# Order of the head-pair projections, and where the stick-breaking output norm takes its squares, in a hybrid attention trunk on one core

## The chip, the core and the metric

The kernel runs on one core of a Trainium2 chip. A core has a matrix engine (PE, with its weight loads shown apart as PEld), a vector engine (DVE), a scalar engine (ACT), a general engine (POOL), and queues that start transfers (most of them SP's). The metric is the time of one execution on the chip in microseconds (us), here the median of three runs.

## The reference

One layer of a streaming encoder works on T = 1088 tokens (1024 of a prompt, 64 of a sample with 128 cached ones). What matters here:

```python
h = rmsnorm(x, g_mix) * (1.0 + scale) + shift            # b_ada, w_ada give scale, shift
q_sb, k_sb, v_sb, q_fx, k_fx, v_fx, logf = split(h @ w_in)  # 8 heads of 64 of each kind
# stick-breaking heads (no softmax)
a = exp(log_sigmoid(z) + cumsum_reverse(log_keep) - log_keep);   o_sb = a @ v_sb
# forgetting heads
p = softmax(mask(q_fx @ k_fx.T / 8 + fq - fk));                  o_fx = p @ v_fx
o = concatenate([rmsnorm(o_sb, g_sb_out), rmsnorm(o_fx, g_fox_out)])   # 512 columns each
x = x + (1.0 + ada[2]) * (o @ w_o)
# then a SwiGLU feed-forward block, a second residual and a last norm
```

The outputs are the new x, the new keys and values of both kinds of heads, and the forget gates. All is in float32.

## The kernel before

**Tiles.** Every float32 operand of a matmul is held as a high and a low part, and a product is three matmuls (L429 high by high, L430 high by low, L431 low by high). Tokens go in three chunks (0 to 383, 384 to 767, 768 to 1087). Heads go in pairs: pairs 0 to 3 are stick-breaking, 4 to 7 forgetting, so that the "sixth pair" is pair index 5.

**A pair.** `project_pair` makes q, then k, then v of a pair (3 chunks x 8 slices of 128 x 3 matmuls each), copies k out for the cache result and its transposes (L501, L507, L512), and returns the raw rows. `values` splits v. `setup` makes of one head the parts the scores take (k2 and kl of k, qs and q2 of q; L572 and L574 are subtractions on POOL).

**Attention.** `attention` takes, for each head and each of nine query blocks, one or two parts of up to 512 keys: the scores (`ps_z`, L689, L692, the mask at L696), for a forgetting head the row maximum (DVE, L717), its negative (L723, L726), the exponential (ACT, L729, which first needs an ACT_TABLE_LOAD where another function was in use), the sum and reciprocal (DVE, L732, L733), the division (POOL, L735), the transposes (PE, `pt_a`, L744), their high part (ACT, L443) and low part (DVE, L750), the product with v (PE, `ps_av`, L753), a fold (DVE, `ot`, L661) and a store to the scratch `oT_d` (SP, L663). A stick-breaking head has two sigmoids (L704), a scan (L708) and a multiplication (POOL, L712) in the place of the softmax. The tiles `a_t`, `o_lo` and the new `o_sq` share one ring of six buffers.

**The stick-breaking norm.** The outputs of pairs 0 to 3 lie in `oT_d` in two halves, since the high and the low part of v give each a sum. `low_job` runs beside each pair; at pair 5 it calls `o_stats` for the three chunks, which loads both halves, adds them (POOL, L824), squares them (ACT, L825) and sums the squares into `sqacc` (POOL, L827, L830). After the first head of pair 6, `sb_early` turns all sums into one column of reciprocal roots (`token_cols`, with matmuls at L204 and a Sqrt at L191, for which ACT loads another table), and calls `sb_norm` for chunks 0 and 2: spread the column over the partitions (L223), load the halves a second time, add them (POOL, L836), scale them (DVE, L900). `sb_ready`, at the start of the attention of pair 7, does chunk 1, splits all three and lets the output projection (`acc_o`, L429 to L431) begin beside the last pair's attention. `squares` (L812) is the sum of squares of the second group norm.

**Order.** The attention of pair n is written ahead of the projections of pair n+1. A list scheduler then sets each engine's order of instructions from a simulated time line; it moves projection matmuls between attention matmuls wherever these would wait. The feed-forward block, from about 850 us, has an order of its own that the change does not touch. Loads and stores sit in SP's queue in the order that the scheduler gives them.

Of the kernel before, what the change touches and what calls it, by code (L numbers as in the profile page):

```python
# [8 lines left out]
F32 = mybir.dt.float32  # L9
# [7 lines left out]
P = 128  # L17
# [72 lines left out]
def f32(ap):  # L90
    return ap.bitcast(F32)
# [3 lines left out]
def tile_hybrid_trunk(  # L95
# [90 lines left out]
    def bank(tag, name):  # L186
        return ps.tile([P, 512], F32, tag=tag, bufs=bank_bufs[tag], name=name)
# [84 lines left out]
    def t_lowraw(dt=F32):  # L272
        return ap1.tile([P, 4, 256], dt, tag="lowraw", name="lowraw")
# [175 lines left out]
    def load_cols(c0):  # L449
        raw, hi, lo = load_w(col_block(w_in[0], c0), KT, P)  # L450
        split(raw, hi, lo, act, pool if c0 in LCP else eng[E_LC[c0 >= 1536]])
        return hi, lo

    def pair_cols(pr):
        return (1536 if pr >= 4 else 0) + (pr % 4) * P

    def load_qk(pr):
        return load_cols(pair_cols(pr)), load_cols(pair_cols(pr) + 512)

    def project(w, evac, tags):  # L460
# [13 lines left out]
    def project_pair(pr, wq, wk):  # L474
        fox = pr >= 4
        p4 = pr % 4
        ck = cache_fox_k if fox else cache_sb_k
        kp, ks = (fox_k_p, fox_k_s) if fox else (sb_k_p, sb_k_s)
        cs = slice(p4 * P, (p4 + 1) * P)
        ptags = PT if pr == 0 else ("acc",) * 9  # L480
        qraw = t_raw(f"qraw{pr}")
        kraw = t_raw(f"kraw{pr}")
        vraw = t_raw(f"vraw{pr}")

        def q_evac(c, t0, n, acc):
            (act.activation(qraw[:, t0:t0 + n], acc[:, :n], AF.Copy, scale=0.125) if E_QE == 'a' else dve.tensor_scalar(out=qraw[:, t0:t0 + n], in0=acc[:, :n], scalar1=0.125, scalar2=None, op0=ALU.mult))

        def k_evac(c, t0, n, acc):
            for a, b, d in kcols(c, t0, n):
                cp(E_KE, kraw[:, d:d + b - a], acc[:, a:b])  # L490

        def v_evac(c, t0, n, acc):
            cp(E_VE, vraw[:, t0:t0 + n], acc[:, :n])

        project(wq, q_evac, ptags[0:3])
        project(wk, k_evac, ptags[3:6])
        wv = load_cols(pair_cols(pr) + 1024)
        kc = ap2.tile([P, P], F32, tag="kc", name="kc")
        sync.dma_start(out=kc, in_=ck[0, 0].rearrange("t h d -> t (h d)")[:, cs])
        pt = bank("acc", "pt_kc")  # L500
        pe.transpose(out=pt[:, 0:P], in_=kc, identity=ident)  # L501
        dve.tensor_copy(out=kraw[:, NP:NP + PAST], in_=pt[:, 0:P])
        kv = kp[0, 0].rearrange("(j p) h d -> p j (h d)", p=P)
        for j0, nj in ((0, 4), (4, 4), (8, 1)):
            pt, st = bank("u", "pt_r"), t_st("kst")
            if nj == 1:
                pe.transpose(out=pt[:NS, 0:P], in_=kraw[:, NP + PAST:KW], identity=ident)  # L507
                act.copy(out=st[:NS, 0:P], in_=pt[:NS, 0:P])
                sync.dma_start(out=ks[0, 0].rearrange("t h d -> t (h d)")[:, cs], in_=st[:NS, 0:P])
                continue  # L510
            for j in range(nj):
                pe.transpose(out=pt[:, j * P:(j + 1) * P], in_=kraw[:, (j0 + j) * P:(j0 + j + 1) * P], identity=ident)  # L512
            cp(E_KS[fox], st, pt)
            sync.dma_start(out=kv[:, j0:j0 + nj, cs], in_=st.rearrange("p (j c) -> p j c", j=nj))
        project(wv, v_evac, ptags[6:9])
        return qraw, kraw, vraw

# [42 lines left out]
            pool.memset(f32(vv[hb][NS:P, 9, :]), 0.0)  # L560
        return vv

    def setup(pr, hb, qraw, kraw, vv):
# [19 lines left out]
        return qs, k2, kl, q2, vv[hb]  # L583

    def forget_gates():

# [224 lines left out]
            act.activation(s_, o[i], AF.Square)  # L811
            add.tensor_tensor(out=acc, in0=acc, in1=s_, op=ALU.add)  # L812

    def o_stats(c, acc):

        t0, n = CH[c]
        for i in range(0, 4, 2):
            both = [
                t_.rearrange("p a b -> p (a b)")[:, 0:2 * n].rearrange("p (k t) -> p k t", k=2)
                for t_ in (t_lowraw(), f32(ap1.tile([P, 4, 256], F32R, tag="ada_l", name="sq_l")))]  # L820
            for k in range(2):
                load_o([t_[:, k] for t_ in both], i + k, t0, n)
            sq = both[0]
            pool.tensor_tensor(out=sq, in0=sq, in1=both[1], op=ALU.add)  # L824
            act.activation(sq, sq, AF.Square)  # L825
            if i == 0:
                pool.tensor_tensor(out=acc, in0=sq[:, 0], in1=sq[:, 1], op=ALU.add)  # L827
            else:
                for k in range(2):
                    pool.tensor_tensor(out=acc, in0=acc, in1=sq[:, k], op=ALU.add)  # L830

    def sum_o(o, k, t0, n, add):

        lo = t_z("o_lo")[:, 0:n]
# [21 lines left out]
    def out_block(g, mp, chunks, hi, lo, evac, tags):  # L856

        wh, wl = wo.pop((g, mp)) if (g, mp) in wo else load_wo(g, mp)
        for c in chunks:
            for m in (2 * mp, 2 * mp + 1):  # L860
# [16 lines left out]
    sb_o = [None] * 3
    sqacc = []
    cols_sb = ap1.tile([P, 2, 9], F32, name="cols_sb")

    def sb_early():

        token_cols([sqacc[0]], [(a, min(P, T - a)) for a in range(0, T, P)], 512, cols_sb)
        for c in SBE:
            sb_norm(c, SBT[c])

    def sb_norm(c, tag):

# [13 lines left out]
        sb_o[c] = o
# [7 lines left out]
    def low_job(pr):  # L910

        for job in JOBS[pr]:
            ada_job(job)
        if pr != 5:
            return lambda: None
        sqacc.append(t_low("sqacc"))
        for c, (t0, n) in enumerate(CH):
            o_stats(c, sqacc[0][:, t0:t0 + n])

        return lambda: None  # L920


    fxh = [[None] * 3 for _ in range(4)]
# [61 lines left out]
        sb_norm(1, SBT[1])  # L985
        sb_split(1)

    low_finish = low_job(0)
    hooks = {6: {0: sb_early}, 7: {HK[0]: fox_first, HK[1]: fox_second}}
    for pr in range(8):  # L990
        if pr < 7:
            wqk = load_qk(pr + 1)
        if pr == 7:
            sb_ready()
        attention(pr, heads, hooks.get(pr, {}))
        if pr < 7:
# [3 lines left out]
            low_finish()  # L1000
# [631 lines left out]
```

## Time and profile before

| | |
|---|---|
| median of three runs | 1619.83 us (1618.46 to 1623.54) |
| the profiled execution | 1622.84 us |
| its span, first to last instruction | 1621.0 us |
| mean granted clock of PE | 0.983 of full speed |
| PE busy | 1537.0 us, 95% |
| DVE, ACT, POOL busy | 1076.9, 782.2, 734.3 us |

The profiled execution takes 1.8 us beyond its span. PE is busy nearly all of the time as a whole, so time is lost only in the stretches where it is not, and a table of windows is the way to them: for each stretch its length, the busy time of every engine with the number of instructions, the clock granted to PE, and the share of the transfer engines. The last product of pair 6's v ends at 587.1 us, the first one of pair 7 begins at 650.4; pair 7's last v product ends at 703.9, and the output projection's first begins at 712.0.

### The profile page before, as it was taken

How to read it: one execution, taken by the hardware profiler on the slowest of the kernel's cores; microseconds unless marked ns; L12 is line 12 of the kernel's file. 1: busy time of each engine (PE TensorE's matmuls, PEld its weight loads, DVE VectorE, ACT ScalarE, POOL GpSimd, SP SyncE). 2: the span in 40 equal slices, each digit the busy share in tenths (PEclk: the TensorE clock that was granted, in tenths of full speed). 3: DMA queues.
4: the chain of work that ended last, by engine and by line, in shares of the span. 5: the costliest groups of instructions: out<-in, count | busy, mean ns of one | idle time of the engine just before them, and what ended most of it. 6: DMA issues, size and time to landing. Idle time of an engine off the chain costs nothing.

```text
span 1621.0 us, 26463 instructions
## 1 busy us (share of the span) xinstructions
PE 1537.0 (95%) x9558; PEld 1440.3 (89%) x9558; DVE 1076.9 (66%) x2121; ACT 782.2 (48%) x1608; POOL 734.3 (45%) x609
## 2 busy tenths in 40 slices
PE   8899999998998976989999999999999999999997
PEld 4698989887887865988999999999899999999997
DVE  5757777688547566557885676667666666666665
ACT  5565665575445554454445445434443333334335
POOL 1556566664657776484453444442222222222222
PEclk9999999999999998999999999999999999999999
DMA  9543434321543454273324554532322121222211
GB/s 302 184 111 92 118 89 122 102 72 24 137 125 104 135 143 112 75 210 94 101 77 138 156 156 145 155 117 66 91 85 61 57 78 53 79 78 78 66 40 79
DMA packets 223202, 174.66 MB, mean 108 GB/s; under 512 B 15488, under 2 KB 213536, under 8 KB 223072
## 3 DMA queue, kind: packets, MB, share of 16 engines
q1 hardware_dynamic: 223072, 172.97, 36.8%
q8 instruction: 76, 1.25, 0.3%
q14 instruction: 54, 0.44, 0.1%
HBM read 138.63 MB, written 27.08 MB: 102 GB/s over the span
## 4 chain that ended last, share of the span: by engine, by line
PE 65%; DVE 7%; DMA 3%; ACT 3%; POOL 2%; issue 2%; SPq 0%; ACTq 0%; DVEq 0%; POOLq 0%
PE gu L1355 19%; PE acc_d L1181 5%; PE acc_d L1183 5%; PE acc_d L1182 5%; PE gu L430 3%; PE gu L431 3%; PE gu L429 3%; PE acc L429 2%; PE acc L430 2%; PE ps_av L753 2%; PE acc L431 2%; PE pt_a L744 2%; PE acc_o L429 2%; PE acc_o L430 2%; PE acc_o L431 2%
## 5 line engine op out<-in xcount | busy, mean ns | idle before, releaser
L1168 ACT CAST whi<-wraw 128x512 fp32r<-128x512 f32 (+1 forms) x209 | 157.1, 776 | 185.3 <-PE acc_d L1183 146.3
L1169 DVE TENSOR_TENSOR wlo<-wraw,whi 128x512 fp32r<-128x512 f32 (+1 forms) x178 | 162.7, 930 | 85.1 <-ACT whi L1168 81.5
L429 PE MATMUL acc<-h,whi 128*128 128x384 f32 (+1 forms) x576 | 199.5, 346 | 4.7 <-ACT vraw L443 2.6
L1204 DVE SCALAR_TENSOR_TENSOR x<-acc_d,ada,x 128x256 f32<-128x256 f32 (+1 forms) x352 | 159.1, 494 | 66.2 <-PE acc_d L1183 65.4
L431 PE MATMUL acc<-h,whi 128*128 128x384 f32 (+1 forms) x576 | 194.2, 337 | 3.8 <-DVE h L406 3.6
L430 PE MATMUL acc<-h,wlo 128*128 128x384 f32 (+1 forms) x576 | 193.9, 337 | 0.0
L1355 PE MATMUL gu<-bT,whi 128*128 128x384 f32 x704 | 187.3, 336 | 0.9 <-ACT u L1369 0.9
L1181 PE MATMUL acc_d<-d,whi 128*128 128x384 f32 (+1 forms) x528 | 175.4, 332 | 3.0 <-DVE h L1284 2.1
L1183 PE MATMUL acc_d<-d,whi 128*128 128x384 f32 (+1 forms) x528 | 173.3, 328 | 0.6 <-DVE d L1517 0.6
L1182 PE MATMUL acc_d<-d,wlo 128*128 128x384 f32 (+1 forms) x528 | 172.8, 327 | 0.0
L443 ACT CAST aT<-pt_a 128x384 fp32r<-128x384 f32 (+3 forms) x208 | 96.8, 475 | 112.1 <-PE pt_a L744 91.8
L750 DVE TENSOR_TENSOR aT<-pt_a,aT 128x384 fp32r<-128x384 f32 (+3 forms) x208 | 110.2, 537 | 41.8 <-ACT aT L443 41.0
L712 POOL TENSOR_TENSOR a_t<-a_t,kp 128x383 f32<-128x383 f32 (+6 forms) x104 | 93.8, 908 | 90.6 <-DVE kp L708 74.8
L1169 POOL TENSOR_TENSOR wlo<-wraw,whi 128x1024 fp32r<-128x1024 f32 x31 | 76.9, 2482 | 125.1 <-ACT whi L1168 121.5
L1323 POOL TENSOR_TENSOR s<-wraw 128x512 f32<-128x512 f32 x22 | 28.6, 1298 | 228.1 <-DMA wraw<-in_w_gate 126.9
L1355 PEld LDWEIGHTS gu<-bT,whi 128*128 128x128 f32 x704 | 128.1, 188 | 1.7 <-ACT u L1369 1.5
L429 PEld LDWEIGHTS acc<-h,whi 128*128 128x128 f32 x576 | 111.8, 194 | 8.3 <-ACT vraw L443 3.1
L744 PE MATMUL pt_a<-ident,a_t 128*128 128x128 f32 x608 | 102.2, 281 | 17.8 <-POOL a_t L735 8.7
L1355 PE MATMUL gu<-bT,wlo 128*128 128x384 f32 x352 | 118.0, 335 | 0.0
L753 PE MATMUL ps_av<-aT,vv 128*128 128x256 f32 x608 | 106.9, 297 | 11.6 <-DVE ot L661 6.0
L431 PEld LDWEIGHTS acc<-h,whi 128*128 128x128 f32 x576 | 111.0, 193 | 5.2 <-DVE h L406 4.9
L430 PEld LDWEIGHTS acc<-h,wlo 128*128 128x128 f32 x576 | 111.5, 194 | 0.5
(357 smaller groups left out, 4200.2 us busy)
## 6 DMA issues: line engine op xcount, KB each, us to landing
wraw<-in_w_gate SPq DMA_DIRECT2D x44, 512.0 KB, 4.1
wraw<-in_w_up SPq DMA_DIRECT2D x44, 512.0 KB, 3.9
wraw<-in_w_down SPq DMA_DIRECT2D x44, 512.0 KB, 3.6
lowraw<-in_w_ada SPq DMA_DIRECT2D x32, 512.0 KB, 3.6
wraw<-in_w_in SPq DMA_DIRECT2D x24, 512.0 KB, 4.5
wa<-in_w_ada SPq DMA_DIRECT2D x16, 512.0 KB, 6.2
oT_d<-ot SPq DMA_DIRECT2D x128, 64.0 KB, 2.0
wraw<-in_w_o SPq DMA_DIRECT2D x11, 512.0 KB, 4.3
```

The source lines that it names most:

```text
L429: pe.matmul(out=acc, lhsT=wh[:, kt, :], rhs=rh[kt], start=st, stop=False)
L430: pe.matmul(out=acc, lhsT=wl[:, kt, :], rhs=rh[kt], start=False, stop=False)
L431: pe.matmul(out=acc, lhsT=wh[:, kt, :], rhs=rl[kt], start=False, stop=sp_)
L744: pe.transpose(out=pt[:, j * P:(j + 1) * P], in_=at[a][:, j * P:(j + 1) * P], identity=ident)
L753: pe.matmul(out=ps_av, lhsT=vv[:, v0 + j, :], rhs=aT[:, j, :], start=(ci == 0 and j == 0), stop=(ci == len(parts) - 1 and j == nb - 1))
L1168: act.copy(out=hi, in_=src)
L1169: lo_eng.tensor_tensor(out=lo, in0=src, in1=f32(hi), op=ALU.subtract)
L1181: pe.matmul(out=a_, lhsT=wh[:, m, :], rhs=dh, start=first, stop=False)
L1182: pe.matmul(out=a_, lhsT=wl[:, m, :], rhs=dh, start=False, stop=False)
L1183: pe.matmul(out=a_, lhsT=wh[:, m, :], rhs=dl, start=False, stop=not first)
L1204: dve.scalar_tensor_tensor(out=xc[:, a:b], in0=acc[:, a:b], scalar=ada[:, 5, m, s:s + 1], in1=xc[:, a:b], op0=ALU.mult, op1=ALU.add)
L1355: pe.matmul(out=acc, lhsT=w_[:, k, :], rhs=bh[BAND[i], k, r_], start=(i in (0, 1, 3) and k == 0 and j == 0), stop=(k == 3 and j == 2), ski ...
```

## The change

- `project_pair` makes k first, then q, then the first head's parts (`setup`), and only then the k outputs and v. The k weights are loaded first. The second head's parts still come after the values.
- `o_stats`, `sqacc`, `cols_sb` and `sb_early` are gone. With them go 48 loads, 6 wide sums and 9 additions on POOL, and 6 squares on ACT.
- `sb_norm` makes the squares of its own chunk from the summed rows: 4 squares on ACT, 3 additions on DVE, the column (3 matmuls, one Sqrt, six small DVE instructions), the spread and the four scalings.
- `sb_norm(0)` hangs behind the first head of pair 5, with wider loads (`load_o2`), `sb_norm(2)` behind that of pair 6; chunk 1 stays at the start of pair 7.

PE issues the same matmuls in both kernels. ACT issues 20 table loads in the place of 16.

```diff
 def load_qk(pr):
-    return load_cols(pair_cols(pr)), load_cols(pair_cols(pr) + 512)
+    wk = load_cols(pair_cols(pr) + 512)
+    return load_cols(pair_cols(pr)), wk
...
-        project(wq, q_evac, ptags[0:3])
-        project(wk, k_evac, ptags[3:6])
+        project(wk, k_evac, ptags[0:3])
         wv = load_cols(pair_cols(pr) + 1024)
...
+        project(wq, q_evac, ptags[3:6])
+        first = setup(pr, 0, qraw, kraw)
...
         project(wv, v_evac, ptags[6:9])
-        return qraw, kraw, vraw
+        return qraw, kraw, vraw, first
...
-    def o_stats(c, acc):
-        t0, n = CH[c]
-        for i in range(0, 4, 2):
...
-            for k in range(2):
-                load_o([t_[:, k] for t_ in both], i + k, t0, n)
-            sq = both[0]
-            pool.tensor_tensor(out=sq, in0=sq, in1=both[1], op=ALU.add)
-            act.activation(sq, sq, AF.Square)
-            if i == 0:
-                pool.tensor_tensor(out=acc, in0=sq[:, 0], in1=sq[:, 1], op=ALU.add)
-            else:
-                for k in range(2):
-                    pool.tensor_tensor(out=acc, in0=acc, in1=sq[:, k], op=ALU.add)
...
-    def sb_early():
-        token_cols([sqacc[0]], [(a, min(P, T - a)) for a in range(0, T, P)], 512, cols_sb)
-        for c in SBE:
-            sb_norm(c, SBT[c])
...
     def sb_norm(c, tag):
         t0, n = CH[c]
-        bc = bank(tag, "bc_o")
-        spread(bc, cols_sb[:, :, 3 * c:3 * c + 3], chunk_toks(c))
...
-        for k in range(4):
-            sum_o(o[k], k, t0, n, pool)
+        if c == 0:
+            for k in (0, 2):
...
+                load_o2(both, k, 0, t0, n)
+                load_o2(lo, k, 1, t0, n)
+                for j in range(2):
+                    pool.tensor_tensor(out=both[:, j], in0=both[:, j], in1=lo[:, j], op=ALU.add)
+        else:
+            for k in range(4):
+                sum_o(o[k], k, t0, n, pool)
+        acc = t_st("o_acc")[:, 0:n]
+        squares(o, acc, [t_z("o_sq")[:, 0:n]], n, dve)
+        col = ap2.tile([P, 2, 3], F32, tag="ss", name="col_o")
+        token_cols([acc], chunk_toks(c), 512, col)
+        bc = bank(tag, "bc_o")
+        spread(bc, col, chunk_toks(c))
         for k in range(4):
             dve.scalar_tensor_tensor(
                 out=o[k], in0=o[k], scalar=go[:, k:k + 1], in1=bc[:, :n], op0=ALU.mult, op1=ALU.mult)
...
-    low_finish = low_job(0)
-    hooks = {6: {0: sb_early}, 7: {HK[0]: fox_first, HK[1]: fox_second}}
+    low_job(0)
+    hooks = {5: {0: lambda: sb_norm(0, SBT[0])}, 6: {0: lambda: sb_norm(2, SBT[2])}, 7: {HK[0]: fox_first, HK[1]: fox_second}}
...
-            heads = [setup(pr + 1, 0, raws[0], raws[1], vv1)]
+            heads = [raws[3] + (vv1[0],)]
...
-            heads.append(setup(pr + 1, 1, raws[0], raws[1], vv1))
+            heads.append(setup(pr + 1, 1, raws[0], raws[1]) + (vv1[1],))
```

What this does to the order shows at three places. The numbers behind names tell copies of a tile apart, and lines of the changed kernel are its own (L744 there is L735 before, L827 is L836, L672 is L663, L753 is L744, L762 is L753).

**POOL where pair 6 goes over to its second head.** `o_8003` and `lowraw` are chunk 0's rows, `o_8037` and `o_3_8038` chunk 2's; `a_t<-a_t,l` are divisions of the attention. Before:

```order
L830 TENSOR_TENSOR sqacc<-sqacc,lowraw 128x320 x2
L836 TENSOR_TENSOR o_8003<-o_8003,o_lo 128x384
L560 MEMSET vv_0_8659 64x128
L836 TENSOR_TENSOR o_8003<-o_8003,o_lo 128x384
L836 TENSOR_TENSOR lowraw<-lowraw,o_lo 128x384 x2
L836 TENSOR_TENSOR o_8037<-o_8037,o_lo 128x320 x3
L735 TENSOR_TENSOR a_t<-a_t,l 128x384
L735 TENSOR_TENSOR a_t<-a_t,l 128x512
L836 TENSOR_TENSOR o_3_8038<-o_3_8038,o_lo 128x320
L735 TENSOR_TENSOR a_t<-a_t,l 128x128
L735 TENSOR_TENSOR a_t<-a_t,l 128x512 x2
```

Now, with chunk 2's rows named `o_7942` and `o_3_7943`:

```order
L710 MEMSET a_t 128x64
L744 TENSOR_TENSOR a_t<-a_t,l 128x512
L744 TENSOR_TENSOR a_t<-a_t,l 128x192
L827 TENSOR_TENSOR o_7942<-o_7942,o_lo 128x320 x3
L827 TENSOR_TENSOR o_3_7943<-o_3_7943,o_lo 128x320
L569 MEMSET vv_0_8602 64x128
L744 TENSOR_TENSOR a_t<-a_t,l 128x384
L744 TENSOR_TENSOR a_t<-a_t,l 128x512 x3
L744 TENSOR_TENSOR a_t<-a_t,l 128x128
L744 TENSOR_TENSOR a_t<-a_t,l 128x256 x2
```

Eight sums stood between the divisions of the two heads, and the two last sums of squares ahead of them; four sums stand there now, and chunk 0's have gone to pair 5.

**SP's queue at the same place**, where `oT_d<-ot` are stores of attention outputs and the loads from `oT_d` bring the norm's rows. Before:

```order
L663 DMA oT_d<-ot 128x64
L141 DMA lowraw<-oT_d 64x384
L141 DMA o_lo<-oT_d 64x384
L141 DMA lowraw<-oT_d 64x384 x2
L141 DMA o_lo<-oT_d 64x384 x2
L141 DMA o_lo<-oT_d 64x320 x2
L141 DMA o_8037<-oT_d 64x320 x2
L141 DMA o_lo<-oT_d 64x320 x2
L141 DMA o_8037<-oT_d 64x320 x2
L141 DMA o_lo<-oT_d 64x320 x4
L663 DMA oT_d<-ot 128x128 x3
```

Now:

```order
L588 DMA klp_691<-nfs_d 64x1216
L672 DMA oT_d<-ot 128x128 x2
L148 DMA o_lo<-oT_d 64x320 x2
L672 DMA oT_d<-ot 128x128
L148 DMA o_lo<-oT_d 64x320 x2
L672 DMA oT_d<-ot 128x128
L148 DMA o_lo<-oT_d 64x320 x2
L672 DMA oT_d<-ot 128x128
L148 DMA o_lo<-oT_d 64x320 x2
L672 DMA oT_d<-ot 128x128 x2
L672 DMA oT_d<-ot 128x64
```

Before, the loads of chunks 0 and 2 stand for the most part behind the first head's last store (`128x64`); now the low halves of chunk 2 stand between the stores, ahead of that one.

**PE ahead of the first product of the output projection**, where pair 7 is the last pair (`k_0`, `qs_0` are its first head's parts, `k_1`, `qs_1` the second's). Before:

```order
L689 MATMUL ps_z<-k_0_8703,qs_0_8702 128x256
L692 MATMUL ps_z<-klp_1085,q_0_8709 128x256
L696 LDWEIGHTS identb
L696 MATMUL ps_z<-mask_fox,identb 128x128
L744 MATMUL pt_a<-ident,a_t 128x128 x3
L551 MATMUL pt_v<-ident,vraw_8391 64x128
L689 MATMUL ps_z<-k_0_8703,qs_0_8702 128x384
L692 MATMUL ps_z<-klp_1085,q_0_8709 128x384
L744 MATMUL pt_a<-ident,a_t 128x128 x4
L429 MATMUL acc_o<-h_0_0_8736,whi 128x384
L430 MATMUL acc_o<-h_0_0_8736,wlo 128x384
L431 MATMUL acc_o<-h_0_1_8737,whi 128x384
```

Now:

```order
L762 MATMUL ps_av<-aT,vv_0_8602 128x256 x5
L230 MATMUL bc_o<-ident,col_o 128x128 x3
L753 MATMUL pt_a<-ident,a_t 128x128 x4
L698 MATMUL ps_z<-k_1_8646,qs_1_8645 128x512
L701 MATMUL ps_z<-klp_693,q_1_8652 128x512
L762 MATMUL ps_av<-aT,vv_0_8602 128x256 x6
L698 MATMUL ps_z<-k_1_8646,qs_1_8645 128x256
L701 MATMUL ps_z<-klp_693,q_1_8652 128x256
L705 LDWEIGHTS identb
L705 MATMUL ps_z<-mask_fox,identb 128x64
L436 MATMUL acc_o<-h_0_0_8668,whi 128x384
L437 MATMUL acc_o<-h_0_0_8668,wlo 128x384
```

Before, 29 matmuls stand between pair 7's last v product and the first `acc_o`, and the first head has only begun; now there are 117, and scores of the second head are among them. Between pair 6's last v product and pair 7's first product there were 240 matmuls and are 285, of which attention's are 225 and 279 (the rest is the norm's), and the divisions on POOL there go from 25 to 30. At the forget gates behind pair 3's projections the same count goes from 89 to 130. A run of 53 attention matmuls behind the first products of the output projection, which had none between them, now has products between them.

## Rows read from the trace of the kernel before

**Rows 1.** The page: busy time, share and instructions of each engine.
```profile
PE 1537.0 (95%) x9558; PEld 1440.3 (89%) x9558; DVE 1076.9 (66%) x2121; ACT 782.2 (48%) x1608; POOL 734.3 (45%) x609
```

**Rows 2.** Windows: start:end, length, busy (count) of each engine, granted clock, DMA.
```profile
500.00:587.10 87.10, 77.93 (x516) 71.04 (x514) 50.16 (x138) 45.05 (x113) 60.92 (x53) 0.96 0.47 127
587.10:626.10 39.00, 31.28 (x202) 24.89 (x201) 32.08 (x97) 26.81 (x75) 37.38 (x41) 0.96 0.49 128
626.10:650.40 24.30, 12.18 (x56) 9.80 (x56) 11.01 (x36) 8.15 (x19) 10.38 (x13) 0.67 0.41 110
587.10:650.40 63.30, 43.46 (x256) 34.69 (x255) 43.08 (x132) 34.97 (x94) 47.76 (x54) 0.85 0.46 121
650.40:703.90 53.50, 50.23 (x323) 48.09 (x323) 22.65 (x57) 21.98 (x52) 29.91 (x26) 0.99 0.45 126
703.90:712.00 8.10, 5.91 (x33) 4.45 (x32) 5.94 (x17) 7.51 (x21) 6.23 (x7) 0.84 0.82 228
712.00:753.90 41.90, 41.64 (x275) 39.24 (x276) 29.78 (x82) 18.91 (x53) 22.72 (x31) 0.99 0.39 117
753.90:764.60 10.70, 8.29 (x53) 6.38 (x53) 8.76 (x25) 6.09 (x18) 6.92 (x8) 0.97 0.45 124
764.60:1621.00 856.40, 841.03 (x5097) 831.34 (x5095) 575.09 (x1017) 360.04 (x634) 273.21 (x175) 1.00 0.31 93
```

**Rows 3.** What PE waited for from 587.1 to 650.4: total us, times, longest.
```profile
PE pt_a L744 <- POOL a_t L735: 6.9, 2, 5.3
PE ps_z L689 <- ACT a_t L729: 6.2, 4, 3.7
```

**Rows 4.** Timeline: start, length, engine, instruction, idle before it, between 628 and 648.
```profile
628.23 1.28 ACT L191 ACT_TABLE_LOAD   x1
...
629.52 0.21 ACT L191 ACTIVATE cols_sb<-cols_sb 128x9 f32<-128x9 f32 x1
...
632.18 0.99 POOL L836 TENSOR_TENSOR o<-o,o_lo 128x384 f32<-128x384 f32 x1 [6.10 <-DMA o<-oT_d]
...
636.04 1.28 ACT L729 ACT_TABLE_LOAD   x1 [4.12 <-DMA o_lo<-oT_d]
...
638.06 0.80 PE L689 MATMUL ps_z<-k,qs 128*128 128x512 f32 x1 [3.67 <-ACT a_t L729]
...
645.67 1.83 POOL L735 TENSOR_TENSOR a_t<-a_t,l 128x384 f32<-128x384 f32 x2
...
646.56 2.11 PE L744 MATMUL pt_a<-ident,a_t 128*128 128x128 f32 x7 [5.29 <-POOL a_t L735]
...
647.46 0.86 POOL L836 TENSOR_TENSOR o<-o,o_lo 128x320 f32<-128x320 f32 x1
```

**Rows 5.** POOL's lines from 587.1 to 650.4: count, busy, mean ns, idle before.
```profile
L735 POOL TENSOR_TENSOR a_t<-a_t,l 128x384 f32<-128x384 f32 (+4 forms) x24 | 18.7, 805 | 1.1 <-DVE l L733 1.1
L836 POOL TENSOR_TENSOR o<-o,o_lo 128x320 f32<-128x320 f32 (+1 forms) x6 | 5.4, 904 | 10.0 <-DMA o<-oT_d 6.1 <-DMA o_lo<-oT_d 3.7 <-DMA oT_d<-ot 0.2
L824 POOL TENSOR_TENSOR lowraw<-lowraw,sq_l 128x640 f32<-128x640 f32 (+1 forms) x3 | 5.0, 1652 | 4.7 <-DMA oT_d<-ot 4.3 <-DMA lowraw<-oT_d 0.4
...
L830 POOL TENSOR_TENSOR sqacc<-sqacc,lowraw 128x384 f32<-128x384 f32 (+1 forms) x4 | 3.7, 934 | 0.2
```

**Rows 6.** DVE's lines from 587.1 to 650.4.
```profile
L750 DVE TENSOR_TENSOR aT<-pt_a,aT 128x384 fp32r<-128x384 f32 (+3 forms) x25 | 13.1, 531 | 2.6 <-ACT aT L443 2.4
L717 DVE TENSOR_REDUCE mx<-ps_z 128x1 f32<-128x384 f32 (+4 forms) x24 | 12.6, 533 | 2.6 <-PE ps_z L696 1.8 <-PE ps_z L692 0.5
...
L900 DVE SCALAR_TENSOR_TENSOR o<-o,cols,bc_o 128x320 f32<-128x320 f32 (+1 forms) x6 | 3.4, 569 | 7.1 <-POOL o L836 7.1
```

**Rows 7.** DVE's lines from 703.9 to 764.6.
```profile
L812 DVE TENSOR_TENSOR sqf<-sqf,sqs 128x320 f32<-128x320 f32 x3 | 2.2, 738 | 0.0
```

**Rows 8.** What PE waited for from 80 to 587.1.
```profile
PE pt_a L744 <- DVE aT L750: 3.8, 3, 2.4
...
PE acc L429 <- ACT vraw L443: 2.6, 1, 2.6
```

More of the change, by code (lines that the diff above doesn't have):

```diff
@@ L135, in tile_hybrid_trunk, with load_o2 @@
     oT_d = spill.tile([KT, 2, 2, HD, T], F32, name="oT_d")
+    def load_o2(t_, k, i, t0, n):
+        for e in range(2):
+            sync.dma_start(
+                out=t_[e * HD:(e + 1) * HD],
+                in_=oT_d[k:k + 2, e, i, :, t0:t0 + n].rearrange("k d t -> d k t"))
     def load_o(tiles, k, t0, n):
@@ L561, in values, with setup @@
         return vv
-    def setup(pr, hb, qraw, kraw, vv):
+    def setup(pr, hb, qraw, kraw):
         fox = pr >= 4
@@ L582, in setup @@
             q2 = None
-        return qs, k2, kl, q2, vv[hb]
+        return qs, k2, kl, q2
     def forget_gates():
@@ L812, in squares @@
             add.tensor_tensor(out=acc, in0=acc, in1=s_, op=ALU.add)
-    def o_stats(c, acc):
-        t0, n = CH[c]
-        for i in range(0, 4, 2):
-            both = [
-                t_.rearrange("p a b -> p (a b)")[:, 0:2 * n].rearrange("p (k t) -> p k t", k=2)
-                for t_ in (t_lowraw(), f32(ap1.tile([P, 4, 256], F32R, tag="ada_l", name="sq_l")))]
-            for k in range(2):
-                load_o([t_[:, k] for t_ in both], i + k, t0, n)
-            sq = both[0]
-            pool.tensor_tensor(out=sq, in0=sq, in1=both[1], op=ALU.add)
-            act.activation(sq, sq, AF.Square)
-            if i == 0:
-                pool.tensor_tensor(out=acc, in0=sq[:, 0], in1=sq[:, 1], op=ALU.add)
-            else:
-                for k in range(2):
-                    pool.tensor_tensor(out=acc, in0=acc, in1=sq[:, k], op=ALU.add)
     def sum_o(o, k, t0, n, add):
@@ L866, in out_block @@
                 evac(m, c, n, acc)
+    lower_k()
     raws = project_pair(0, *load_qk(0))
@@ L871, in tile_hybrid_trunk @@
             spill_x(c)
-    lower_k()
     vv0 = values(0, raws[2])
-    heads = [setup(0, hb, raws[0], raws[1], vv0) for hb in range(2)]
+    heads = [raws[3] + (vv0[0],), setup(0, 1, raws[0], raws[1]) + (vv0[1],)]
     x1 = [[None] * 3 for _ in range(KT)]
     sb_o = [None] * 3
-    sqacc = []
-    cols_sb = ap1.tile([P, 2, 9], F32, name="cols_sb")
-    def sb_early():
-        token_cols([sqacc[0]], [(a, min(P, T - a)) for a in range(0, T, P)], 512, cols_sb)
-        for c in SBE:
-            sb_norm(c, SBT[c])
     def sb_norm(c, tag):
         t0, n = CH[c]
-        bc = bank(tag, "bc_o")
-        spread(bc, cols_sb[:, :, 3 * c:3 * c + 3], chunk_toks(c))
         if c < 2:
-            o = [t_[:, a:a + n] for t_ in (t_low("o32"), t_lowraw().rearrange("p a b -> p (a b)")) for a in (0, n)]
+            oo = (t_low("o32"), t_lowraw().rearrange("p a b -> p (a b)"))
+            o = [t_[:, a:a + n] for t_ in oo for a in (0, n)]
         else:
@@ L896, in sb_norm @@
             o = [t_[:, a:a + n] for a in (0, n, 2 * n)] + [ap1.tile([P, n], F32, tag="small", name="o32_3")]
-        for k in range(4):
-            sum_o(o[k], k, t0, n, pool)
+        if c == 0:
+            for k in (0, 2):
+                both = oo[k // 2][:, 0:2 * n].rearrange("p (k t) -> p k t", k=2)
+                lo = ap1.tile([P, 4, 256], F32, tag="ada_l", name="o_lo").rearrange("p a b -> p (a b)")
+                lo = lo[:, 0:2 * n].rearrange("p (k t) -> p k t", k=2)
+                load_o2(both, k, 0, t0, n)
[11 more added lines that the diff above has]
+        spread(bc, col, chunk_toks(c))
         for k in range(4):
@@ L913, in low_job @@
             ada_job(job)
[L914 to L920, printed above, removed]
     fxh = [[None] * 3 for _ in range(4)]
@@ L998, in tile_hybrid_trunk @@
             vv1 = values(pr + 1, raws[2])
-            heads = [setup(pr + 1, 0, raws[0], raws[1], vv1)]
-            low_finish()
+            heads = [raws[3] + (vv1[0],)]
             if pr == FG:
                 forget_gates()
-            heads.append(setup(pr + 1, 1, raws[0], raws[1], vv1))
-            low_finish = low_job(pr + 1)
+            heads.append(setup(pr + 1, 1, raws[0], raws[1]) + (vv1[1],))
+            low_job(pr + 1)
     def evac_sb(m, c, n, acc):
```

## The prediction

> **What bounds the kernel now.** I began with the page: PE is busy 95% of the span [rows 1], so what a change can gain is PE's idle time, in the stretches that have some. The windows give those stretches [rows 2]. Behind 764.6 us there are 15.4 us without PE in 856.4, and the change does not reach there. The worst stretch is 587.1 to 650.4: no projection product runs in it, and PE is busy for 43.46 of 63.30 us, so 19.8 us are idle. Next to it, 650.4 to 703.9, with pair 7's products, has 3.3 us idle. Inside the worst stretch the loss is concentrated: 626.1 to 650.4 has 12.18 us of PE in 24.30, and a granted clock of 0.67, while neighbours have 0.96 and 0.99. Then I asked what PE waited for there: two waits for POOL's divisions, 6.9 us, and four for ACT's exponentials, 6.2 us [rows 3], together 13.1 us. The timeline shows their common source [rows 4]. POOL's eight sums of the norm run from 632.18 to 648.3, each waiting for a load, the first 6.10 us. The second head's divisions are queued behind seven of them: the first two run at 645.67, and PE's transposes of their result start at 646.56, after 5.29 us of nothing. The exponential at 636.04 pays a table load of 1.28 us behind the Sqrt of 629.52, and PE stands 3.67 us for its ring buffer. So this stretch is bound by a queue on POOL that waits for loads, and the low clock follows the idle PE.
>
> **A. Pair 6 into pair 7 (587.1 to 703.9): -15 us.** Before, this took 63.3 + 53.5 = 116.8 us. Removed are the rest of the squares' pass (on POOL 5.0 us of wide sums and 3.7 of additions, with 4.7 us of waits for loads [rows 5]) and four of the eight sums at the junction. The four that stay, for chunk 2, have their low halves' loads earlier in SP's queue, ahead of the first head's last store. Added are the norm's own squares on DVE, and more attention: 54 more attention matmuls now lie between the last v product of pair 6 and the first product of pair 7, and divisions go from 25 to 30. These matmuls leave the next stretch, where they had lain beside products.
>
> With POOL's queue out of the way, which engine is next? POOL had 47.76 us in the stretch and loses about 5.0 + 3.7 + 4 x 1.0 = 12.7, gaining 5 x 0.8 = 4, so some 39. PE's own work is 43.46 plus 54 matmuls of 0.152 us (41.90 us over 275 in the stretch where PE is full [rows 2]), some 52, part of which is the low clock's (0.67 made matmuls longer). DVE had 43.08 us, of which eight scalings at 0.57 take 4.6 (six of them in [rows 6]). The remaining 38.5 over 25 divisions are 1.54 us for each, its casts included; the maximum and the low part of the transposes, 0.53 us each, are the largest [rows 6]. For 30 that is 46.2. Three additions of squares at 0.74 [rows 7] add 2.2, four scalings 2.3: a floor of 51 us on DVE, much like PE's. Dependences are never covered entirely; I take 55. The next stretch gives up 54 x 0.152 = 8.2 us at most. I count 7, since those matmuls filled gaps there: 46.5. Together 101.5, against 116.8: -15. Bounds: -20 where DVE's floor and the full 8.2 hold (51 + 45.3 = 96.3). At the other end the four remaining sums still hold up the second head: only half of the 12.1 us that PE lost in 626.1 to 650.4 comes back (-6), five more divisions cost 5 x 1.54 = 8, the chain of squares 3, and the next stretch returns 7: -2. I take -15, near the floor, because the rows put 13.1 us of PE's wait on this one queue.
>
> **B. Chunk 0's norm beside pair 5, and the squares' pass out of it (500 to 587.1): -1 us.** PE has 9.2 us idle in 87.1 [rows 2]; products of pair 6 fill it. Four sums at 1.0 us, four squares, a Sqrt with two table loads of 1.28, three additions of 0.74 us and four scalings come in; a part of the pass's sums and additions goes. Neither DVE (50 of 87) nor ACT (45) is full; POOL (61) is relieved. What hides the new chain is the products beside it. Without that cover it would hold the second head for its two table loads and three additions, 5 us; at the other end two thirds of the 9.2 idle go, 6. I take -1, since most of that idle time is not POOL's.
>
> **C. k first, first head's parts before v, at the other boundaries: 0 us.** The first head's scores can start while v is still being made, so PE has both kinds of work earlier; what it uses earlier it lacks later. The waits that this could shorten are single ones: 3.8 us in three times on the low part, 2.6 on a v copy [rows 8]; all together gone would give 6. Against that the run without products at the forget gates goes from 89 matmuls to 130: 41 at the pure stretch's 63.30/256 = 0.247 instead of 0.152 are 3.9 us, and each boundary moves the head's subtractions on POOL, and its transfers in SP's queue, ahead of the k outputs, which I put at 2; +6. The ends are symmetric, and no row favours one, so 0.
>
> **D. Start of the last pair: +4 us.** 703.9 to 712.0, with 29 matmuls before the output projection, becomes a run of 117. The 88 extra at the rate of 587.1 to 626.1, 39.0/202 = 0.193, instead of 0.152, cost 3.6. Chunk 1's own squares and Sqrt now stand in that run: two table loads, 2.6, of ACT. In return the run of 53 attention matmuls from 753.9 on (8.29 of 10.70 us) is spread among products: -2.4. Sum +3.8. Bounds: -2.4 if only that counts; at 0.247 for each the 88 cost 8.4, with 2.6 of table loads and 1 of additions +12. The nearer row is the stretch where a first head runs with POOL busy but not stopped, the former.
>
> **Sum.** -15 - 1 + 0 + 4 = -12. The profiled execution took 1622.84 us (span 1621.0 and 1.8 outside), so 1610.8 there. It lies 3.0 above the median of the runs shown, and the difference carries over: 1619.83 - 12 = 1608.
>
> **A rule against it.** The rows show a table load as 1.28 us, with the Sqrt's answer at 629.52, right behind its load of 628.23 [rows 4]. The change adds four such loads, 5.1 us of ACT, an engine that is half idle, and two of them are in D. The Trainium skill ("ScalarE: Activation LUTs", "Table sets: the hidden batching unit") says that activations should be grouped by table set, all exponentials and then all roots; the change spreads the roots over three places. In "What ACT_TABLE_LOAD costs" it gives a switch 1283 ns of load and some 1380 ns of drain; by that the four would cost an estimated 10.6 us, and were all of the further 5.5 on the path, the sum would be -6.5. The load agrees with the row; no drain is seen there.
>
> **Rivals.**
> *More than that (0.16).* A reaches its floor (-20), and the earlier scores take half of the waits of [rows 8] (-3), with D at 0: -24, 1596 us. For it: every row puts the loss on one queue. Against: longer runs without products seldom come to their floor.
>
> *No change (0.18).* The four sums that stay still stand ahead of the second head's first division and wait for their loads, so A is -5, B is 0 and D +4: -1, 1619 us. For it: in [rows 4] the wait is for loads rather than for the sums themselves, and chunk 2's high halves and stores still share SP's queue. Against: those loads stand earlier now.
>
> *Slower (0.18).* The halt moves to the start of the last pair. It has no products either, now 117 matmuls, and the chunk-1 chain (loads, four sums on POOL, squares, Sqrt, spread, scalings, splits) is what the output projection waits for. At the rate of 626.1 to 650.4, 24.30/56 = 0.434 us, the 88 matmuls cost 88 x (0.434 - 0.152) = 24.8, less 2.4 of the spread run: +22.4, with 2.6 of table loads +25. With A at -15 and B at -1 that is +9: 1629 us. It decides where PE idles over 16 us more than before between pair 7's last v product and the first product of the output projection. For it: the clock fell to 0.84 in the 8.1 us there already. Against: POOL is not blocked by loads for chunks 0 and 2 in that place.
>
> **How the numbers follow.** The forecast, with A near its floor and D small, has 0.48 and its own range of 1603 to 1614. A difference under 0.3%, 4.9 us, is what a measurement of this kernel cannot tell from none: 1615.0 to 1624.7 is "same". Faster is 0.48 + 0.16 = 0.64, same 0.18, slower 0.18. The range reaches from the better case's 1596 over the forecast and the no-change case to 1624; the slower case and the tail of the better one stay out, some 0.2.
>
> **What will show it.** A: the stretch from pair 6's last v product to pair 7's first product at 52 to 58 us although it holds 54 more matmuls, with no PE wait for L735's successor over 3 us, and a granted clock over 0.85; wrong if POOL's four sums there wait over 6 us together. B: PE idle from 500 us to pair 6's last v product near 9 us. D: between pair 7's last v product and the first `acc_o` some 25 us, of which PE idles 5 to 8; over 24 of idle time is the slower rival. C: PE's idle time up to the start of pair 5's attention changed by less than 6 us. A wait for the ring of `a_t` behind a low half's load, or stores of `ot` late behind such loads in SP's queue, would upset A.

## The result: slower by 0.8%

The changed kernel takes 1634.29 us (median of four runs, 1631.22 to 1639.99), the kernel before 1619.14 beside it: a ratio of 1.0079, 95% interval 1.006 to 1.0099. Forecast was 1608 in 1596 to 1624. The profiled execution of the changed kernel took 1634.02 us with a span of 1632.2; the one of before had 1621.0, so the two traces show 11.2 of the 15 us (the profiled execution of before lay 3.7 above its median). All windows below are of one execution each. Two traces whose orders of instructions agree up to the last v product of pair 7 (the changed kernel, and its run with another bank below) lie 4.4 us apart there, so sums of windows are good to some 4 us, while medians are firmer.

The page of the changed kernel, to be read against [rows 1]: its span and busy times.

```profile
span 1632.2 us, 26345 instructions
...
PE 1546.8 (95%) x9558; PEld 1445.0 (89%) x9558; DVE 1099.7 (67%) x2142; ACT 790.2 (48%) x1620; POOL 714.3 (44%) x594
```

The matmuls are as many as before, yet PE is busy for 9.8 us longer: much of the loss is the low clock, not standing still. Now the windows of the changed kernel (columns as in [rows 2]). They are cut by work, not by time: pair 2's projections; pair 3's last v product to pair 4's first product; pair 5's projections; two short pieces of these, which overlap; pair 6's last v product to pair 7's first product; pair 7's projections; from there to the first product of the output projection; to the end of attention; to the end of the stick-breaking half of the output projection; to the last block's start.

```profile
188.60:264.60 76.00, 72.55 (x482) 65.23 (x482) 57.34 (x94) 45.69 (x100) 47.81 (x42) 0.98 0.36 101
333.10:372.20 39.10, 34.46 (x233) 26.68 (x231) 34.52 (x59) 28.47 (x74) 23.62 (x29) 1.00 0.28 75
443.10:513.10 70.00, 64.92 (x419) 58.98 (x417) 35.76 (x95) 32.67 (x79) 44.77 (x37) 0.95 0.38 105
467.40:473.40 6.00, 5.56 (x18) 5.22 (x19) 1.65 (x5) 0.59 (x1) 2.78 (x1) 0.50 0.71 173
467.50:475.00 7.50, 7.11 (x27) 6.74 (x28) 1.55 (x4) 0.59 (x1) 2.78 (x1) 0.58 0.74 187
...
594.20:651.30 57.10, 45.33 (x292) 35.75 (x291) 48.27 (x150) 40.91 (x113) 37.42 (x44) 0.94 0.32 86
651.30:698.90 47.60, 45.94 (x283) 42.96 (x281) 20.75 (x41) 16.10 (x35) 24.82 (x20) 1.00 0.51 144
698.90:729.70 30.80, 23.28 (x123) 18.62 (x123) 22.34 (x67) 24.11 (x64) 21.68 (x28) 0.78 0.52 155
729.70:779.60 49.90, 49.49 (x330) 47.92 (x330) 41.92 (x103) 22.27 (x57) 26.67 (x29) 1.00 0.40 112
779.60:804.00 24.40, 22.03 (x118) 21.03 (x116) 14.81 (x42) 5.70 (x12) 3.39 (x2) 0.86 0.12 35
804.00:823.30 19.30, 15.42 (x88) 14.53 (x89) 15.20 (x24) 7.24 (x12) 9.51 (x4) 0.91 0.27 85
```

The same pieces of before, where [rows 2] has not got them:

```profile
188.10:268.70 80.60, 76.06 (x516) 68.87 (x515) 60.34 (x103) 48.83 (x110) 52.40 (x46) 0.98 0.36 104
337.60:368.60 31.00, 29.70 (x208) 23.77 (x206) 26.38 (x47) 24.47 (x62) 18.71 (x24) 1.00 0.24 67
440.20:502.40 62.20, 60.92 (x409) 55.62 (x407) 32.06 (x87) 30.32 (x72) 41.71 (x35) 1.00 0.40 115
502.90:587.10 84.20, 75.03 (x494) 68.49 (x494) 48.57 (x135) 43.03 (x110) 59.15 (x53) 0.96 0.49 131
712.00:786.50 74.50, 71.83 (x458) 67.29 (x459) 56.03 (x151) 34.35 (x90) 39.48 (x47) 0.97 0.41 119
786.50:796.10 9.60, 9.60 (x64) 9.36 (x63) 7.67 (x19) 2.59 (x6) 2.10 (x1) 1.00 0.22 71
796.10:812.00 15.90, 14.65 (x99) 14.20 (x100) 14.57 (x32) 8.71 (x15) 9.20 (x4) 1.00 0.34 100
```

Three sums come out of the two tables. Up to pair 6's last v product the changed kernel is 594.2 - 587.1 = 7.1 us behind. From there to pair 7's last v product it takes 57.1 + 47.6 = 104.7 in place of 116.8: 12.1 ahead. From there to the last block it takes 30.8 + 49.9 + 24.4 + 19.3 = 124.4 in place of 8.1 + 74.5 + 9.6 + 15.9 = 108.1: 16.3 behind. Together +11.3. Of the 16.3, half is idle PE (14.2 us against 6.1), and half is about as many matmuls (656 and 649 in the records) at clocks of 0.78, 0.86 and 0.91.

The gain lies where it was argued for. What PE waited for in the pair 6 stretch has lost its two large entries of [rows 3]; these are now the longest wait of PE there, and the largest total of POOL:

```profile
PE pt_a L753 <- POOL a_t L744: 3.1, 1, 3.1
```

```profile
POOL o L827 <- DMA o_lo<-oT_d: 5.1, 4, 1.8
```

The loss behind pair 7's last v product is a chain. From the timeline of the changed kernel (start, length, engine, instruction), chunk 1's norm at the last pair, from its last sums to the output projection:

```profile
703.84 1.95 POOL L827 TENSOR_TENSOR lowraw<-lowraw,o_lo 128x384 f32<-128x384 f32 x2
...
714.97 0.54 DVE L821 TENSOR_TENSOR o_acc<-o_acc,o_sq 128x384 f32<-128x384 f32 x1
...
715.57 0.83 PE L211 MATMUL pc<-ones,o_acc 128*128 128x1 f32 x6
...
717.68 1.28 ACT L198 ACT_TABLE_LOAD   x1
...
718.98 0.21 ACT L198 ACTIVATE col_o<-col_o 128x3 f32<-128x3 f32 x1
...
719.21 0.18 DVE L199 RECIPROCAL col_o<-col_o 128x3 f32<-128x3 f32 x1 [0.73 <-ACT col_o L198]
...
725.15 0.15 DVE L203 TENSOR_TENSOR col_o<-col_o 128x3 f32<-128x3 f32 x1
...
726.52 0.83 PE L230 MATMUL bc_o<-ident,col_o 128*128 128x128 f32 x6
...
728.44 1.13 DVE L899 SCALAR_TENSOR_TENSOR lowraw<-lowraw,cols,bc_o 128x384 f32<-128x384 f32 x2
...
729.72 0.41 PE L436 MATMUL acc_o<-h,whi 128*128 128x384 f32 x1 [0.49 <-DVE l L741]
```

From 705.8 to 729.6 it takes 23.8 us. Its own instructions are short; the five small ones on DVE, four of them under 0.2 us, stretch from 719.21 to 725.30 since each takes its turn in a queue full of attention. The first product of the output projection starts 0.15 us after the last scaling has read the spread. It needs chunk 0 alone, but the spread `bc_o` of chunk 1 and the first block's `acc_o` use the same single bank ("acc": `SBT = ('u', 'acc', 'acc')`, and the first entry of `OT` is "acc"), in the order written. Before, the first product stood behind the last scaling in the same way, and the spread held the bank even longer, 7.3 us in place of 3.1 (726.52 to 729.57). But the column was there long since, so the spread could start right behind pair 7's last v product:

```profile
704.61 0.89 PE L223 MATMUL bc_o<-ident,cols_sb 128*128 128x128 f32 x6
...
711.29 0.60 DVE L900 SCALAR_TENSOR_TENSOR lowraw<-lowraw,cols,bc_o 128x384 f32<-128x384 f32 x1
...
711.95 0.69 PE L429 MATMUL acc_o<-h,whi 128*128 128x384 f32 x1 [0.32 <-DVE lowraw L900]
```

Counted from the last v product, the spread starts after 27.6 us now, and started after 0.7 before.

### The profile page after: what moved, and what is told of

Its sections match the earlier page's. It is cut to its first block, busy times and chain, and to the rows that moved or that the text cites. A ratio compares the mean times of both kernels' runs of the same rounds, so it can differ in the third digit from the quotient of the medians.

```text
span 1632.2 us, 26345 instructions
## 1 busy us (share of the span) xinstructions
PE 1546.8 (95%) x9558; PEld 1445.0 (89%) x9558; DVE 1099.7 (67%) x2142; ACT 790.2 (48%) x1620; POOL 714.3 (44%) x594
## 4 chain that ended last, share of the span: by engine, by line
PE 76%; DVE 12%; ACT 5%; DMA 3%; issue 3%; POOL 1%; SPq 0%; DVEq 0%; ACTq 0%; POOLq 0%
PE gu L1346 18%; PE acc_d L1172 5%; PE acc L436 5%; PE acc_d L1174 5%; PE acc_d L1173 5%; PE acc L437 5%; PE acc L438 5%; PE gu L437 3%; PE gu L438 3%; PE gu L436 3%; PE ps_av L762 3%; PE pt_a L753 3%; PE ps_z L698 2%; PE pa L789 2%; PE pa L380 1%
## 5 line engine op out<-in xcount | busy, mean ns | idle before, releaser
L753 PE MATMUL pt_a<-ident,a_t 128*128 128x128 f32 x608 | 103.6, 281 | 17.7 <-DVE aT L759 8.6
L762 PE MATMUL ps_av<-aT,vv 128*128 128x256 f32 x608 | 108.2, 299 | 7.3 <-DVE ot L670 4.4
```

What stands on the lines that cost most here:

```text
L753: pe.transpose(out=pt[:, j * P:(j + 1) * P], in_=at[a][:, j * P:(j + 1) * P], identity=ident)
L762: pe.matmul(out=ps_av, lhsT=vv[:, v0 + j, :], rhs=aT[:, j, :], start=(ci == 0 and j == 0), stop=(ci == len(parts) - 1 and j == nb - 1))
```

## The experiments

All were timed in five rounds beside the kernel before, whose median was 1621.3 us in the first four and 1621.83 in the others. "At the last product" is the difference from before at the end of pair 7's v, "at the last block" the one at the start of the first product that reads `fo_k`, in the forgetting half of the output projection (812.0 us before), and what the last pair costs is the second less the first.

**The order alone.** The kernel before, with the hunks on `load_qk`, `project_pair` and `setup`; `lower_k()`, which these parts need, moves ahead of pair 0's projections, as it does in the changed kernel (cut here):

```diff
-        project(wq, q_evac, ptags[0:3])
-        project(wk, k_evac, ptags[3:6])
+        project(wk, k_evac, ptags[0:3])
...
+        project(wq, q_evac, ptags[3:6])
+        first = setup(pr, 0, qraw, kraw)
```

> Only the order of the projections is changed (k, q, first head's parts, k outputs, v); the squares' pass and the early norm of before stay. Theory 1 (the norm's own chain for chunk 1 holds the last pair, the order costs the 7 to 10 us ahead of pair 6): the last pair's start is as before (27 matmuls without products against 29), the stretches up to the end of pair 6's projections are 7 to 10 us longer, so about 1627 us. Rival 2 (the new order alone lets the last pair run out of products): about 1634 us, with 20 us or more before the first product of the output projection. Rival 3 (the order is worth nothing): 1619 us.

1628.71 us, ratio 1.0038 (1.0025 to 1.0051). Its windows: the forget gates, pair 5's and pair 6's projections, the last pair's start.

```profile
334.50:375.00 40.50, 35.85 (x233) 27.77 (x231) 34.61 (x59) 28.51 (x74) 23.51 (x29) 0.96 0.26 72
446.30:515.50 69.20, 64.12 (x419) 58.39 (x416) 36.18 (x96) 32.99 (x80) 45.09 (x37) 0.95 0.38 106
517.00:594.90 77.90, 72.25 (x483) 65.89 (x481) 47.90 (x127) 39.89 (x101) 59.48 (x52) 0.98 0.53 142
...
712.20:721.40 9.20, 4.97 (x30) 3.28 (x28) 6.30 (x16) 7.87 (x21) 9.03 (x10) 1.00 0.67 193
```

The order loses at the same places as the changed kernel: 40.5 and 69.2 us (before 31.0 and 62.2), less 6.3 in pair 6's, +8.3 at the last product. The last pair starts as before, and costs nothing (+6.2 at the last block). Theory 1 holds, rivals 2 and 3 fall. In the instruction streams, the moved `setup` is no part of it: with q, k and the first head's parts ahead of v, the order on PE, DVE, ACT and POOL is that of before, and with k, q and the parts left behind the values it is that of this run; only a few transfers in SP's queue change places. So k ahead of q makes the whole difference on the engines.

**The norm alone.** The changed kernel with q, k, v and both `setup` calls as before:

```diff
-        project(wk, k_evac, ptags[0:3])
+        project(wq, q_evac, ptags[0:3])
+        project(wk, k_evac, ptags[3:6])
...
-        project(wq, q_evac, ptags[3:6])
-        first = setup(pr, 0, qraw, kraw)
```

> Only the norm is changed (own squares, chunk 0 beside pair 5, chunk 2 beside pair 6); the projections keep the order q, k, v and both heads' parts behind the values. Theory 1: the last pair's start is as bad as in the changed kernel (138 matmuls without products), +16 us, the pair 6 stretch gains 12, chunk 0 beside pair 5 gains up to 3: 1618 to 1623 us, with 25 us or more before the first product of the output projection. Rival 2 (it is the order): the last pair starts as in before, and the gain of 12 is left: about 1606 us.

1628.19 us, 1.0035 (1.0022 to 1.0048): slower than before, and than theory 1's range; rival 2's 1606 falls. It is 8.6 us ahead at the last product and 4.0 behind at the last block. The windows of pair 6 into pair 7, and from the last product on:

```profile
583.90:644.40 60.50, 46.43 (x301) 37.69 (x299) 51.89 (x155) 41.83 (x118) 39.53 (x47) 0.94 0.31 81
644.40:695.30 50.90, 45.20 (x280) 42.84 (x281) 17.66 (x39) 17.53 (x37) 26.42 (x22) 1.00 0.47 130
695.30:725.90 30.60, 23.65 (x146) 18.51 (x144) 24.77 (x76) 24.86 (x68) 19.45 (x26) 0.89 0.56 169
725.90:774.40 48.50, 45.47 (x290) 44.27 (x291) 35.18 (x92) 20.03 (x50) 24.08 (x26) 0.96 0.39 108
774.40:799.90 25.50, 22.95 (x136) 21.94 (x134) 18.14 (x47) 5.96 (x12) 3.40 (x2) 0.94 0.13 38
799.90:816.00 16.10, 13.47 (x88) 12.95 (x88) 10.82 (x16) 6.23 (x9) 9.54 (x4) 0.99 0.31 99
```

The last pair loses 12.6 us without the order: 30.6 us before the first product, and 25.5 us of products without attention at the end. Theory 1 named the place; its gain of 12 in pair 6 did not come: 60.5 + 50.9 = 111.4 us in place of 116.8 is 5.4. The medians of the two halves come near the whole, 7.4 + 6.9 = 14.3 us of the 15.2 (13.0, set against the later median of 1621.3), but the stretches do not add up: pair 6 into pair 7 gains 5.4 with the norm alone, loses 0.5 with the order alone, and gains 12.1 with both; the last pair costs 12.6, -2.1 and 16.3. Nothing in the stretches explains that the sums nearly agree.

**The changed kernel with another bank for one spread.**

```diff
-SBT = ('u', 'acc', 'acc')
+SBT = ("u", "u", "acc")
```

> The changed kernel, with chunk 1's spread in the bank of the value transposes in place of the output projection's only bank. Theory 1 (the first products of the output projection stand behind chunk 1's spread in one bank): the first 48 products come some 20 us earlier and fill attention, 91 matmuls without products are left behind them; half of the 16 us at the last pair goes, about 1626 us. Rival 2 (the products are late for their own rows, not for the bank): 1634 us as before the edit.

1623.73 us, 1.0016 (1.0005 to 1.0028): theory 1 holds, with more than the half that it gave, and rival 2 falls. The last product is 0.6 ahead, the last block 4.3 behind: the last pair costs 4.9 us in place of 16.3. So two thirds of its loss were one bank. PE's work without products is not gone: 91 matmuls stand behind the first 48 products, where chunk 1 is wanted.

**Chunk 1's squares in a pass beside pair 5**, in the changed kernel:

```diff
+        if pr == 5:
+            acc = t_low("sqacc")[:, 0:CH[1][1]]
+            o_stats(1, acc)
+            token_cols([acc], chunk_toks(1), 512, col1)
```

> The changed kernel, with chunk 1's squares in a pass of their own beside pair 5 (loads, sums, squares, column and Sqrt there), so that at the last pair chunk 1 has only loads, sums, spread and scalings. Theory 1: the first product of the output projection comes within 12 us of the last v product (27 matmuls between), and the 16 us of the last pair go; the pass costs 1 to 3 us beside pair 5: about 1620 us, all that stays is the order's cost less the gain at pair 6. Rival 2 (the last pair's loss comes from the order or the low clock): 1630 us or more.

1628.75 us, 1.0046 (1.0029 to 1.0063). Pair 6's stretch and the last pair's start:

```profile
593.30:665.10 71.80, 53.16 (x337) 43.48 (x336) 60.41 (x180) 47.45 (x130) 41.02 (x52) 0.90 0.29 78
...
713.80:722.70 8.90, 5.53 (x31) 3.61 (x29) 6.30 (x16) 7.88 (x21) 8.90 (x10) 0.87 0.62 184
```

The last pair is mended as theory 1 said: 8.9 us to its first product, and from +10.0 at the last product to +7.6 at the last block, so that it costs -2.4 in place of 16.3. But pair 6's stretch grows from 57.1 to 71.8, with 45 more matmuls in it and DVE busy for 60.41. The count says that products were used up earlier; what the extra pass holds up there beside that was not taken apart. The time of 1620 was missed, and the gain of A with it; rival 2's 1630 was for a last pair that stays slow, which it did not.

**The norm alone, with that bank.** As the norm alone, with the one-line edit above.

> The norm's change alone (projections in the old order), with chunk 1's spread in the bank of the value transposes. The norm alone was 8.6 us ahead of before at the last v product of pair 7 and lost 12.6 behind it. Theory 1 (the loss there is chunk 1's chain, ahead of the output projection in its one bank): 48 products come before the chain is through, 92 matmuls without products are left, the loss falls to about 5: some 1616 to 1618 us beside 1621 of before. Rival 2 (the loss at the end is the price of the attention done early, whatever the bank): still +5 to +7.

1615.56 us, 0.9966 (0.9953 to 0.9978): faster than both kernels, and a little better than theory 1. From the first product to the last block:

```profile
696.30:769.90 73.60, 69.41 (x463) 63.76 (x463) 61.17 (x174) 44.14 (x114) 42.54 (x52) 1.00 0.49 142
769.90:786.10 16.20, 15.34 (x99) 15.11 (x99) 10.32 (x31) 3.44 (x7) 3.42 (x2) 1.00 0.16 50
786.10:804.80 18.70, 15.72 (x95) 15.03 (x94) 16.29 (x28) 8.82 (x15) 9.85 (x4) 0.91 0.29 90
```

It is 8.3 us ahead at the last product and 7.2 at the last block, so the last pair costs 1.1 us in place of 12.6. The clock is 1.00 to the end of attention. With the same bank the new order took 2.4 us more than before, the old one takes 6.3 less: the order costs 8.7 us here, and 7.4 alone.

**Two other banks** for the same spread, "t" (two of the attention's transposes) and "av" (its outputs):

```diff
-SBT = ("u", "u", "acc")
+SBT = ("u", "t", "acc")     # the other run: "av"
```

> As the run before, with chunk 1's spread in one of the two banks of the attention's transposes: 144 products of the output projection stand ahead of the halt, and 72 matmuls without products behind them. Theory 1: the loss behind pair 7's last v product falls to 0 to 3 us, 1613 to 1616 us; rival (holding a transposes' bank slows the attention instead): 1618 us or more.

> As the run before, with chunk 1's spread in the single bank of the attention's outputs: 144 products ahead of the halt, 64 matmuls without products behind. Theory 1: as the run before, 1613 to 1617 us; rival (the outputs wait behind the spread, one after another): 1620 us or more.

1625.09 us (1.0022, 1.0012 to 1.0031) and 1626.43 (1.0033, 1.0021 to 1.0045). Theory 1 is wrong here and the times are the rivals': though 144 products stand ahead of the halt and fewer matmuls behind it, the last pair costs 9.5 and 11.7 us. The stretch from the first product to the end of attention takes 92 to 94 us in place of 73.6 (with some 30 matmuls more in it), and PE now waits for the chain itself. In the timeline of the run with "t":

```profile
710.03 0.83 PE L211 MATMUL pc<-ones,o_acc 128*128 128x1 f32 x6 [3.53 <-DVE o_acc L819]
```

That is one wait of several; whether the rivals' mechanisms make the rest was not taken apart. Counting matmuls without products was a poor forecast of time: which bank the spread takes counts as well.

**The order alone, with the cached keys' transpose in another bank.**

```diff
-        pt = bank("acc", "pt_kc")
+        pt = bank("u", "pt_kc")
```

> The order's change alone, with the transpose of the cached keys in the value transposes' bank in place of the projections' bank. Theory C1 (k first costs 8 us in pair 5's projections since that transpose waits in the projections' one bank for k's copy on DVE, and PE's clock falls behind it): pair 5's projections take 62 to 64 us in place of 69 to 70, and the run without products at the forget gates (96 matmuls in place of 130) 33 to 36 us in place of 40: 1619 to 1622 us, the order alone being 7 above before. Rival C2 (the products are used up earlier and lack later, wherever this transpose is): 1627 us or more.

1626.18 us, 1.0026 (1.001 to 1.0042), overlapping the interval of the order alone. Pair 3's projections, the gates and pair 5's projections:

```profile
258.40:333.70 75.30, 68.87 (x449) 63.46 (x448) 48.98 (x77) 40.53 (x90) 38.72 (x38) 0.95 0.34 99
333.70:380.00 46.30, 40.32 (x250) 31.18 (x248) 39.31 (x68) 32.52 (x80) 26.46 (x33) 0.89 0.29 72
449.20:515.40 66.20, 63.34 (x426) 57.71 (x425) 35.52 (x99) 34.95 (x80) 48.44 (x37) 1.00 0.41 115
```

Pair 5 falls from 69.2 to 66.2 us at a clock of 1.00: C1's wait was part of it, though less than C1's 62 to 64. But while pair 2's projections get 3.5 us faster, pair 3's get 8.7 slower (66.6 in the order alone) and the gates 5.8 slower: 46.3, where C1 had 33 to 36. The time lies just below C2's 1627, so C2 holds for the sum, and C1 for one stretch.

## Why the prediction was wrong

Forecast was -12, and the traces show +11.3, a miss of 23.3 us. Of this A makes 2.9, B and C together 8.1 (7.1 behind at pair 6's last v product, where -1 was forecast), and D 12.3.

**A was right in kind, and its size in part by luck.** Forecast -15, measured -12.1 in the changed kernel. The halt behind the sums is gone with its low clock (0.94 where before had 0.85), DVE is the fullest engine with 48.27 of 57.10 us, and the 54 matmuls left the next stretch, which fell by 5.9. The four sums that stay wait 5.1 us for their low halves, less than the 6 set as the bound; PE's longest wait for a division is 3.1, just over the 3 that its sign allowed. But the sum laid nearly all of it to POOL's queue, which the norm alone clears as well, for a gain of 5.4. The rest comes only with both halves of the change; why stays open.

**B was too small.** With the norm alone, pair 6's projections fell from 84.2 to 79.2 us: -5, inside its bounds (-6 to +5), where -1 was taken. The order alone shortens the same stretch by 6.3, and both together by 4.6, so they draw on the same idle time.

**C failed.** "No row favours one, so 0" stood for what is +7.8 us at pair 6's last v product with the order alone, beyond the bound of +6. Two places make it. At the gates the stretch between pair 3's and pair 4's products takes 8 us more, with 3.3 more of idle PE, and has 25 more matmuls; pair 2's projections had been 4.6 us shorter, with 34 matmuls fewer. So the counts say that what is used early is paid for there. In pair 5, in the timeline of the changed kernel, k's last chunk is through by 463 us, its copy stands in DVE's queue behind a cast and several small instructions, and the next matmul in the bank, the transpose of the cached keys, waits for it and starts 0.1 us behind its end:

```profile
465.03 1.86 DVE L283 TENSOR_SCALAR sc<-ada 128x16 f32<-128x16 f32 x1
466.81 0.54 DVE L452 COPY kraw<-acc 128x256 f32<-128x256 f32 x2
...
467.45 0.45 PE L508 MATMUL pt_kc<-ident,kc 128*128 128x128 f32 x1 [3.66 <-issue]
```

That is 3.66 us of nothing on PE, and then 7.5 us at a granted clock of 0.58, about 3 us more. The trace does not name what PE waited for ("issue"); that it was the bank is what the last run speaks for, where the wait is gone. The prediction spoke of the first head's parts, whose place changes the order of no compute engine; it is k ahead of q that moves the instructions.

**D is the step that lost the case.** "+4", bounds -2.4 to +12; measured +16.3 (12.6 with the norm alone). The rate of 0.193 came from the row of 587.1 to 626.1, the wrong neighbour, which does not end at a product that stands behind one long chain; 30.8/123 is 0.250. What the term left out: the first output product stands behind chunk 1's spread in one bank, so that it starts only when the whole chain is through, 30.8 us after the last product; and the products not used beside attention run alone later, 24.4 us in place of 9.6. The edit of the bank alone takes back 11.4 of the 16.3, and 11.5 of the 12.6; the squares moved out of the chain take back all. D's own sign in the forecast, some 25 us to the first product with PE idle for 5 to 8, came out at 30.8 and 7.5 and did not give the loss away. The forecast let some 17 us more up to that product come back all but 4; measured, 22.7 us more came back all but 16.3.

**The slower rival** named the place (start of the last pair, chunk 1's chain) and came to 1629 us; it got 0.18. Its test was wrong: PE idles only 5.3 us more before the first product, not over 16. The rest was lost as a low clock and behind the attention. The rule of the Trainium skill that the prediction held against the change ("ScalarE: Activation LUTs", "Table sets: the hidden batching unit": all exponentials first, then all roots) did not decide it: there are four more loads of 1.28 us, and the Sqrt's answer at 718.98 comes right behind its load; the load in the chain is 1.3 of its 23.8 us.

What stays open: why the scheduler's order at the gates takes 25 matmuls more when k is first, why the gain of A needs both halves of the change, and by what way the order costs the last pair some 4 us (4.9 with the other bank, 1.1 with the other bank and the old order; the traces are no finer than that).

## What to carry to other kernels

When a step moves a small chain of dependent instructions into a stretch where engines work in order, price its turns in the queues, not its instructions; and look at which bank or buffer it holds meanwhile, and who is next in it. Filler used earlier is filler missing later, so follow a gain to the end of the stretch that shares the filler before it is counted.

## What was not expected of the hardware

A wait of 3.66 us, with PE at full clock before it, was followed by 7.5 us at a granted clock of 0.58; 6.0 of them ran at 0.50, the lower of PE's two levels (1.2 of 2.4 GHz). So a single wait cost nearly twice its length. In the last pair, half of a loss of 16.3 us was PE busy for longer with as many matmuls, in stretches at 0.78, 0.86 and 0.91, with no wait of PE over 2.1 us in it.
